# Attention rows of the second token half: one merged row of 128 scores in place of 256

## The chip, the cores and the metric

The kernel runs on one NeuronCore of a Trainium2 chip. Five engines work side by side, each through its own queue in order: TensorE (PE in the profile, with its weight loads as PEld), VectorE (DVE), ScalarE (ACT), GpSimd (POOL) and SyncE (SP, which issues most DMAs). They meet through semaphores only. The metric is device time in microseconds (us); less is better. A time is the median of several runs; the profile is one more execution, taken by the hardware profiler.

## The reference, cut to what matters

Two layers over 256 tokens of width 2048: a Mamba-2 mixer and then a sliding-window attention with 32 query heads of 64 channels, 4 shared key/value heads, a window of 128 and one sink per head. Both end in a layer norm of `ALPHA * x + mixer(x)`. The change touches the attention alone:

```python
def _swa_sink_attention(q, k, v, sinks):
    bsz, seqlen, hk, rq, hd = q.shape
    nb = seqlen // WINDOW                                   # 2 blocks of 128
    ...
    kk = jnp.concatenate([jnp.pad(kb, pad)[:, :-1], kb], axis=2)   # block before, own block
    vv = jnp.concatenate([jnp.pad(vb, pad)[:, :-1], vb], axis=2)
    s = jnp.einsum("bcqhrd,bckhd->bchrqk", qb, kk).astype(jnp.float32) * (hd ** -0.5)
    qi = jnp.arange(WINDOW)[:, None] + WINDOW
    ki = jnp.arange(2 * WINDOW)[None, :]
    diff = qi - ki
    ...
    valid = (diff >= 0)[None] & (diff < WINDOW)[None] & (kpos >= 0)
    s = jnp.where(valid[None, :, None, None], s, -jnp.inf)
    ...
    m = jnp.maximum(jnp.max(s, axis=-1, keepdims=True), sk)
    p = jnp.exp(s - m)
    p = p / (jnp.sum(p, axis=-1, keepdims=True) + jnp.exp(sk - m))
    o = jnp.einsum("bchrqk,bckhd->bcqhrd", p.astype(vv.dtype), vv)
```

For a query at place q of the second half (tokens 128 to 255), a key at place k of its own block is valid where k <= q, and a key at place k of the block before is valid where k > q. So exactly 128 of the 256 scores of a row are valid, and for each k exactly one of the two blocks holds the valid one. The first half has only its own block.

## The kernel before, in words

All matmul operands are float32, and the large products are made of three matmuls each: weights and activations are split into a high part and a remainder, and high*high, high*low and low*high are added up in PSUM (`mac`, `x_stat`, `out_unit`). Weights arrive as units of 128x2048 floats in two DMAs; ScalarE writes the high part of each half (L135), VectorE the remainder (L136). `next_unit` loads two units ahead of use.

The first layer takes the span up to about 690 us and is not touched. The second starts with K and V (x_stat, then `ktr` turns K), then follows a list of steps `B_ORDER` over the four KV heads j: "q" (`q_block`, four units, L744 to L746), "g" (`gate_block`, four units of 48 matmuls each, L208), "o" (`out_unit`, four units of 24 matmuls each, L268 to L270). The output units of the last head come at the very end, followed by the layer norm.

The attention itself is cut into small steps which are laid between these units by a list written out by hand: `later(n, fn)` puts a step on the list, and each unit ends in `tick()`, which counts the list down and emits the steps that are due, in their order on the list. For head j the steps are: `qtr` (turn the rotated queries, L799), `attend(j, 0)` (first token half), and from inside it `turn_p` after 3 ticks, `pv` after 6 and `attend(j, 1)` after 3. `attend(j, 1)` asks for its own `turn_p` after 3 ticks and `pv` after 4. For the last head, `pv` of the first half comes after 4 ticks and `attend(3, 1)` after 1. The tile framework then puts the instructions of each engine in an order, mainly the program's, and adds the semaphore waits.

`attend(j, h)` works on 128 queries of 8 query heads. It makes scores with two tiles of PSUM at a time (L836, two rows of 64 partitions each, for even and odd heads), adds the mask while copying them to SBUF (L841, VectorE), takes the row maximum (L849), combines it with the sink (L850 to L852), runs eight exponentials on ScalarE, each with a row sum (L855), adds the sink's share (L858), inverts (L859) and multiplies all weights by it (L860). `turn_p` transposes the weights on TensorE, four 128x128 blocks to a PSUM tile (L869), and copies each tile to SBUF, on ScalarE (L874) for odd heads and VectorE (L876) for even ones. `pv` multiplies V with them (L883), applies the gate (L889) and splits the result (L898, L899) for the output units.

For h = 1 the row has 256 scores: L836 has 256 columns per head, `p1` is 128x8x256, and L869 runs 16 times per head j, into four PSUM tiles.

The PSUM ring `ax` has four tiles of 128x512 and serves all of these small steps: scores, transposes and the product with V. The ring `pt` in SBUF has four tiles too. `mask_a1` (columns 640 to 895 of the constants `cc`) is the mask of the second half, `mask_a0` (768 to 895) that of one's own block: 0 where k <= q and -1e30 elsewhere. Columns 256 to 383 of `cc` hold an upper triangle of ones, `tri` in `_layout`.

Of the kernel before, what the change touches and what calls it, by code (L numbers as in the profile page):

```python
# [8 lines left out]
F32 = mybir.dt.float32  # L9
F32R = mybir.dt.float32r  # L10
I32 = mybir.dt.int32
AF = mybir.ActivationFunctionType
ALU = mybir.AluOpType
AX = mybir.AxisListType

P = 128
# [29 lines left out]
NEG = -1.0e30  # L46
# [15 lines left out]
def trunk(ctx: ExitStack, tc: tile.TileContext, A: dict, out: bass.AP, dbg=None):  # L62
    nc = tc.nc
# [16 lines left out]
    def nm(s):  # L80
        uid[0] += 1
        return f"{s}_{uid[0]}"
# [4 lines left out]
    def ax_tile():  # L87
        return ax_ps.tile([P, 512], F32, tag="ax", name=nm("ax"), bufs=4)

    cc = cst.tile([P, 896], F32, tag="cc", name="cc")  # L90
    ident = cc[:, 0:128]
    ones = cc[:, 128:256]
    mask_ssd = cc[:, 256:640]
    mask_a1 = cc[:, 640:896]
    mask_a0 = cc[:, 768:896]
    pc = cst.tile([P, PC_END], F32, tag="pc", name="pc")
    eps_t = cst.tile([P, 1], F32, tag="eps", name="eps_t")
# [532 lines left out]
    for g in range(NG):  # L630
        t = 10 * g
# [84 lines left out]
    bp = pool("bp")  # L716
# [106 lines left out]

    def attend(j, h):

        nk = P * (h + 1)
        q2 = qT[j, h]
        p = bp.tile([P, 8, nk], F32, tag=f"p{h}", name=nm("p"), bufs=1)
        mask = mask_a1 if h else mask_a0
        per = 512 // nk  # L830
        for b in range(0, 4, per):
            pss = [ax_tile(), ax_tile()]
            for i in range(per):
                for par in range(2):
                    rows = slice(64 * par, 64 * par + 64)
                    nc.tensor.matmul(  # L836
                        pss[par][:, i * nk : (i + 1) * nk], q2[rows, b + i, :], kT[rows, j, :nk],
                        start=True, stop=True,
                    )
            for par in range(2):  # L840
                nc.vector.tensor_tensor(  # L841
                    p[:, par * 4 + b : par * 4 + b + per, :],
                    pss[par][:].rearrange("p (a k) -> p a k", a=per),
                    mask.unsqueeze(1).to_broadcast([P, per, nk]), ALU.add,
                )
        sk = snk[:, j * 8 : j * 8 + 8]
        sm = bp.tile([P, 8, 8], F32, tag="sm", name=nm("sm"), bufs=2)
        mx, ng, rs, es, ri = [sm[:, i, :] for i in range(5)]
        nc.vector.tensor_reduce(mx, p[:], AX.X, ALU.max)  # L849
        nc.vector.tensor_tensor(mx, mx, sk, ALU.max)  # L850
        nc.vector.tensor_scalar(ng, mx, -1.0, None, ALU.mult)
        nc.vector.tensor_tensor(es, sk, ng, ALU.add)  # L852
        nc.scalar.activation(es, es, AF.Exp)
        for r in range(8):
            nc.scalar.activation(  # L855
                p[:, r, :], p[:, r, :], AF.Exp, bias=ng[:, r : r + 1], accum_out=rs[:, r : r + 1]
            )
        nc.vector.tensor_tensor(rs, rs, es, ALU.add)  # L858
        nc.vector.reciprocal(ri, rs)  # L859
        nc.vector.tensor_tensor(p[:], p[:], ri.unsqueeze(2).to_broadcast([P, 8, nk]), ALU.mult)  # L860

        pts = {}

        def turn_p():
            for kc in range(h + 1):
                for par in range(2):
                    pt = ax_tile()
                    for a in range(4):
                        nc.tensor.transpose(  # L869
                            pt[:, a * P : (a + 1) * P], p[:, par * 4 + a, kc * P : (kc + 1) * P], ident  # L870
                        )
                    t = bp.tile([P, 512], F32, tag="pt", name=nm("pt"), bufs=4)
                    if par:
                        nc.scalar.copy(t[:], pt[:])  # L874
                    else:
                        nc.vector.tensor_copy(t[:], pt[:])  # L876
                    pts[kc, par] = t

        def pv():
            ov = ax_tile()  # L880
            for kc in range(h + 1):
                for par in range(2):
                    nc.tensor.matmul(  # L883
                        ov[64 * par : 64 * par + 64, :], vt[:, kc, j * 64 : j * 64 + 64], pts[kc, par][:],
                        start=kc == 0, stop=kc == h,
                    )
            o = bp.tile([P, 4, P], F32, tag="o", name=nm("o"), bufs=1)
            hs = slice(h * P, (h + 1) * P)
            nc.vector.scalar_tensor_tensor(  # L889
                o[:], ov[:].rearrange("p (a t) -> p a t", a=4), 0.5, sg[j][:, :, hs], ALU.mult, ALU.mult  # L890
            )
            if j not in os_:
                os_[j] = (
                    bp.tile([P, 4, S], F32R, tag="oH", name=nm("oH"), bufs=2),
                    bp.tile([P, 4, S], F32R, tag="oL", name=nm("oL"), bufs=2),
                )
            oH, oL = os_[j]
            nc.scalar.activation(oH[:, :, hs], o[:], AF.Copy)  # L898
            nc.vector.tensor_tensor(oL[:, :, hs], o[:], oH[:, :, hs].bitcast(F32), ALU.subtract)  # L899

        last = j == 3
        later(3, turn_p)
        later(4 if last or h else 6, pv)
        if h == 0:
            later(1 if last else 3, lambda: attend(j, 1))
# [65 lines left out]
def _layout(inputs):  # L971
    import numpy as np

    f = {k: np.asarray(v) for k, v in inputs.items()}
    c = np.ascontiguousarray
    a = {}
    x = f["x"][0]
    a["xt"] = c(x.T.reshape(KT, P, S).transpose(1, 0, 2))
    a["xk"] = c(x.reshape(2, P, D).transpose(1, 0, 2))

    def wstat(w):
        k, n = w.shape
        return c(w.reshape(k // P, P, n // P, P).transpose(2, 1, 0, 3).reshape(n // P, P, k))

    def xstat(w, per, n):
        k, m = w.shape
        return c(
            w.reshape(k // (per * P), per, P, m // n, n).transpose(3, 0, 2, 1, 4).reshape(-1, P, per * n)
        )

    w = f["a_w_in"][0]
    o_xs, o_b, o_c, o_dt = DI, 2 * DI, 2 * DI + 1024, 2 * DI + 2048
    order = []
    for g in range(NG):
        blk = [o_b + g * P, o_c + g * P]
        blk += [o_xs + g * 512 + i * P for i in range(4)]
        blk += [g * 512 + i * P for i in range(4)]
        order += [blk[k] for k in (BLOCKS0 if g == 0 else BLOCKS)]
    cols = np.concatenate([np.arange(s, s + P) for s in order])
    a["wa"] = wstat(w[:, cols])  # L1000
    wdt = w[:, o_dt:].reshape(KT, P, NHD).transpose(1, 0, 2)
    a["first"] = np.concatenate([a.pop("xt"), a["wa"][0].reshape(P, KT, P), wdt], 2)
    conv = np.concatenate([f["a_conv_w"][0], f["a_conv_b"]], 0)
    corder = []
    for g in range(NG):
        corder += [o_b - DI + g * P, o_c - DI + g * P] + [g * 512 + i * P for i in range(4)]
    cv = np.stack([conv[:, s : s + P] for s in corder], 0).transpose(2, 0, 1).reshape(P, 240)
    dsk = np.repeat(f["a_d"][0], 64).reshape(32, P).T
    nw = f["a_norm_w"][0].reshape(32, P).T
    two = lambda v: np.concatenate([v, v])[:, None]  # L1010
    a["pc"] = c(np.concatenate([cv, dsk, nw, two(f["a_dt_bias"][0]), two(f["a_log"][0])], 1))
    wo = f["a_w_out"][0]
    a["wo"] = xstat(wo, 4, 512).reshape(4, NG, P, 2048).transpose(1, 0, 2, 3).reshape(32, P, 2048)
    a["lng"], a["lnb"] = f["ln_g"], f["ln_b"]
    a["wkv"] = xstat(f["kv_w"], 4, 512)
    a["kvb"] = f["kv_b"]
    wi = f["b_w_in"][0]
    a["wq"] = xstat(wi[:, :D], 4, 512)
    a["wg"] = wstat(wi[:, D:])
    a["qb"] = f["b_q_bias"][0]  # L1020
    a["snk"] = f["b_sinks"][0].reshape(4, 4, 2).transpose(0, 2, 1).reshape(32)
    wb = f["b_w_out"][0]
    a["wb"] = xstat(wb, 4, 512).reshape(4, 4, P, 2048).transpose(1, 0, 2, 3).reshape(16, P, 2048)
    a["pos"] = c(f["positions"][0].reshape(2, P).T)
    inv = (np.float64(500000.0) ** (-np.arange(0, 16, 2) / 16.0)).astype(np.float32)
    a["inv"] = np.tile(inv[None], (P, 1))
    i = np.arange(P)
    cc = np.zeros((P, 896), np.float32)
    cc[:, 0:128] = np.eye(P)
    cc[:, 128:256] = 1.0  # L1030
    tri = (i[None, :] >= i[:, None]).astype(np.float32)
    cc[:, 256:384] = tri
    cc[:, 384:512] = 1.0
    cc[:, 512:640] = tri
    cc[:, 640:768] = np.where(i[None, :] > i[:, None], 0.0, NEG)
    cc[:, 768:896] = np.where(i[None, :] <= i[:, None], 0.0, NEG)
    a["cc"] = cc
    return {k: c(v) for k, v in a.items()}
# [20 lines left out]
```

## Time and profile before

| | |
|---|---|
| median of 3 runs | 1021.66 us (1019.65 to 1025.03) |
| profiled execution, time | 1019.52 us |
| profiled execution, span from first to last instruction | 1017.7 us |
| granted TensorE clock, mean | 0.998 |
| HBM read | 195.41 MB, 194 GB/s over the span |
| transposes of weights, L869 | 96, of which 64 in the second halves |
| scores, L836 | 128 matmuls, 64 of 128 columns and 64 of 256 |

A line of the groups reads: source line, engine, operation, output <- inputs, shapes, count, then busy time in us and the mean of one in ns, then the idle time of the engine before them and what ended it. A line of the stretches gives, for each engine, its busy time in that window in us and its number of instructions. Matmul records overlap, so a record's length is not what it takes from the queue; the distance from one start to the next is.

### The profile page before, as it was taken

To read this page: it belongs to the slowest core of one execution; us is meant where nothing else is said; L and a number is where in the kernel's file an instruction comes from. 1 tells how busy PE (TensorE), PEld (TensorE's weight loads), DVE (VectorE), ACT (ScalarE), POOL (GpSimd) and SP (SyncE) were. 2 spreads that over 40 slices of the span, in tenths; PEclk is the share of its full clock that TensorE was granted. 3 is DMA by queue.
4 is the path that set the end of the run, shared out by engine and by line. 5 is a ranking of instruction groups with operands and counts; after the bars stand their busy time and mean duration, and the time that the engine had idled before them with its cause. 6 is when DMAs were issued, how large, how long until landed. Compare 5 with 4: busy or idle time off the path is not lost.

```text
span 1017.7 us, 17576 instructions
## 1 busy us (share of the span) xinstructions
PE 1001.8 (98%) x7012; PEld 900.8 (89%) x7012; DVE 772.2 (76%) x1099; ACT 560.5 (55%) x917; POOL 89.8 (9%) x112
## 2 busy tenths in 40 slices
PE   8999999999999999999999999999999999999997
PEld 6999989999999998998999998868988879879875
DVE  5869887966786886786786786897567875775876
ACT  6686846647646655654664663545455453453632
POOL 0000303004003003001200301201000000000002
PEclk9999999999999999999999999999999999999999
DMA  8797676565675666666666456647545545545522
GB/s 318 265 289 250 192 248 203 175 226 168 201 225 186 215 204 187 214 207 194 200 199 207 156 194 193 245 148 237 179 164 176 163 141 179 177 137 180 203 84 83
DMA packets 57794, 198.79 MB, mean 195 GB/s; under 512 B 6304, under 2 KB 10928, under 8 KB 56944
## 3 DMA queue, kind: packets, MB, share of 16 engines
q1 hardware_dynamic: 56352, 191.61, 58.0%
q0 software_dynamic: 1072, 5.53, 1.5%
q8 instruction: 55, 0.90, 0.3%
q10 hardware_dynamic: 288, 0.52, 0.1%
q14 instruction: 27, 0.22, 0.1%
HBM read 195.41 MB, written 2.23 MB: 194 GB/s over the span
## 4 chain that ended last, share of the span: by engine, by line
PE 77%; DVE 9%; ACT 5%; DMA 5%; issue 3%; POOL 1%; SPq 0%; ACTq 0%; DVEq 0%; POOLq 0%
PE mm L208 40%; PE mm L268 7%; PE mm L269 7%; PE mm L270 7%; PE mm L744 3%; PE mm L745 3%; PE mm L746 3%; DVE wl L136 3%; ACT wh L135 2%; DMA wr<-in_wa 2%; DVE cv L389 1%; PE ax L506 1%; DMA rb<-rscr 1%; PE ax L836 1%; PE ax L883 1%
## 5 line engine op out<-in xcount | busy, mean ns | idle before, releaser
L136 DVE TENSOR_TENSOR wl<-wr,wh 128x1024 fp32r<-128x1024 f32 (+2 forms) x342 | 398.3, 1181 | 132.3 <-ACT wh L135 131.1
L135 ACT ACTIVATE wh<-wr 128x1024 fp32r<-128x1024 f32 (+2 forms) x342 | 337.4, 1011 | 237.4 <-PE mm L208 74.3
L208 PE MATMUL mm<-xH,wh 128*128 128x256 f32 x1280 | 356.6, 279 | 2.2 <-DVE cv L389 1.8
L208 PE MATMUL mm<-xH,wl 128*128 128x256 f32 x1280 | 355.0, 277 | 1.5 <-DVE wl L136 1.5
L208 PE MATMUL mm<-xL,wh 128*128 128x256 f32 x1280 | 354.9, 277 | 0.0
L208 PEld LDWEIGHTS mm<-xH,wh 128*128 128x128 f32 x1280 | 241.0, 188 | 6.8 <-issue 2.6
L208 PEld LDWEIGHTS mm<-xH,wl 128*128 128x128 f32 x1280 | 240.9, 188 | 2.1 <-DVE wl L136 1.9
L208 PEld LDWEIGHTS mm<-xL,wh 128*128 128x128 f32 x1280 | 241.1, 188 | 0.9
L268 PE MATMUL mm<-wh,yH 128*128 128x512 f32 x256 | 101.4, 396 | 0.0
L269 PE MATMUL mm<-wh,yL 128*128 128x512 f32 x256 | 99.9, 390 | 0.0
L270 PE MATMUL mm<-wl,yH 128*128 128x512 f32 x256 | 99.7, 389 | 0.0
L522 POOL TENSOR_TENSOR yz<-yz,z 128x256 f32<-128x256 f32 x32 | 32.9, 1037 | 523.3 <-DVE yz L517 523.3
L389 DVE SCALAR_TENSOR_TENSOR cv<-mm,pc,cv 128x255 f32<-128x255 f32 x144 | 68.6, 476 | 6.4 <-ACT cv L387 5.0
L208 PE MATMUL mm<-x1H,wh 128*128 128x256 f32 x256 | 71.9, 281 | 0.0
L208 PE MATMUL mm<-x1H,wl 128*128 128x256 f32 x256 | 71.0, 277 | 0.0
L208 PE MATMUL mm<-x1L,wh 128*128 128x256 f32 x256 | 71.0, 277 | 0.0
L744 PE MATMUL mm<-wh,x1H 128*128 128x512 f32 x160 | 63.3, 396 | 0.0
L745 PE MATMUL mm<-wh,x1L 128*128 128x512 f32 x160 | 62.7, 392 | 0.2 <-DVE x1L L708 0.2
L746 PE MATMUL mm<-wl,x1H 128*128 128x512 f32 x160 | 62.6, 391 | 0.3 <-DVE wl L136 0.2
L268 PEld LDWEIGHTS mm<-wh,yH 128*128 128x128 f32 x256 | 48.1, 188 | 10.3 <-DVE z L459 1.0
L270 PEld LDWEIGHTS mm<-wl,yH 128*128 128x128 f32 x256 | 48.1, 188 | 10.1
L269 PEld LDWEIGHTS mm<-wh,yL 128*128 128x128 f32 x256 | 48.1, 188 | 9.0
(183 smaller groups left out, 1312.5 us busy)
## 6 DMA issues: line engine op xcount, KB each, us to landing
wr<-in_wa SPq DMA_DIRECT2D x158, 512.0 KB, 5.0
wr<-in_wo SPq DMA_DIRECT2D x64, 512.0 KB, 4.6
wr<-in_wq SPq DMA_DIRECT2D x32, 512.0 KB, 4.3
wr<-in_wg SPq DMA_DIRECT2D x32, 512.0 KB, 4.7
wr<-in_wb SPq DMA_DIRECT2D x32, 512.0 KB, 4.5
rb<-rscr SPq DMA_DIRECT2D x16, 512.0 KB, 5.6
el<-rscr SPq DMA_DIRECT2D x16, 256.0 KB, 5.0
wr<-in_wkv SPq DMA_DIRECT2D x8, 512.0 KB, 5.2
```

Of the source, the lines that this page charges most:

```text
L135: nc.scalar.activation(h[:, sl], v, AF.Copy)
L136: nc.vector.tensor_tensor(l[:, sl], v, h[:, sl].bitcast(F32), ALU.subtract)
L208: m = nc.tensor.matmul(ps, a, b, start=first and i == 0, stop=last and i == 2)
L268: nc.tensor.matmul(ps[:], aH[:, k, hs], u.h[:, ks], start=k == 0, stop=False)
L269: nc.tensor.matmul(ps[:], aL[:, k, hs], u.h[:, ks], start=False, stop=False)
L270: nc.tensor.matmul(ps[:], aH[:, k, hs], u.l[:, ks], start=False, stop=k == 3)
L389: nc.vector.scalar_tensor_tensor(a[:, sft:], ps[:, : S - sft], w(3 - sft), a[:, sft:], ALU.mult, ALU.add)
L506: nc.tensor.matmul(ps[64 * r : 64 * r + 64, cols], xd[:, c, r, :], e[:, 256:] if c else e[:, :256], start=c == 0, stop=c == 1,)
L522: nc.gpsimd.tensor_tensor(v, v, st.z[i][:], ALU.mult)
L744: nc.tensor.matmul(ps[:], x1H[:, kk, hs], u.h[:, ks], start=kk == 0, stop=False)
L745: nc.tensor.matmul(ps[:], x1L[:, kk, hs], u.h[:, ks], start=False, stop=False)
L746: nc.tensor.matmul(ps[:], x1H[:, kk, hs], u.l[:, ks], start=False, stop=kk == KT - 1)
```

## The change

For the second token half, `p1` shrinks to 128x8x128. The scores are still made for both key blocks. ScalarE copies those of one's own block from PSUM into `p`, and VectorE then copies those of the block before over them wherever `mask_a0` is not zero (k > q): `copy_predicated` with the mask's bits as condition. Maximum, exponentials and scaling run over 128 places. `turn_p` transposes 8 blocks in place of 16 into two PSUM tiles, and VectorE copies each tile twice, once times `1 - tri` (the weights of the block before) and once times `tri` (those of one's own block), so that `pv` has the same four tiles and the same eight matmuls (four with each block's V) as before. The first half keeps its instructions; only the order of the loops in `turn_p` is turned round. In the constants, `1 - tri` takes the place of the first half of `mask_a1`.

```diff
-    mask_a1 = cc[:, 640:896]
+
+    tri, anti = cc[:, 256:384], cc[:, 640:768]
     mask_a0 = cc[:, 768:896]
...
-        p = bp.tile([P, 8, nk], F32, tag=f"p{h}", name=nm("p"), bufs=1)
-        mask = mask_a1 if h else mask_a0
+        p = bp.tile([P, 8, P], F32, tag=f"p{h}", name=nm("p"), bufs=1)
...
             for par in range(2):
-                nc.vector.tensor_tensor(
-                    p[:, par * 4 + b : par * 4 + b + per, :],
-                    pss[par][:].rearrange("p (a k) -> p a k", a=per),
-                    mask.unsqueeze(1).to_broadcast([P, per, nk]), ALU.add,
+                v = p[:, par * 4 + b : par * 4 + b + per, :]
+                if h == 0:
+                    nc.vector.tensor_tensor(
+                        v, pss[par][:].rearrange("p (a k) -> p a k", a=per),
+                        mask_a0.unsqueeze(1).to_broadcast([P, per, P]), ALU.add,
+                    )
+                    continue
+                two = pss[par][:].rearrange("p (a c k) -> p a c k", a=per, c=2)
+
+                nc.scalar.copy(v, two[:, :, 1, :])
+                nc.vector.copy_predicated(
+                    v, mask_a0.bitcast(U32).unsqueeze(1).to_broadcast([P, per, P]), two[:, :, 0, :]
                 )
...
-        nc.vector.tensor_tensor(p[:], p[:], ri.unsqueeze(2).to_broadcast([P, 8, nk]), ALU.mult)
+        nc.vector.tensor_tensor(p[:], p[:], ri.unsqueeze(2).to_broadcast([P, 8, P]), ALU.mult)
...
         def turn_p():
-            for kc in range(h + 1):
-                for par in range(2):
-                    pt = ax_tile()
-                    for a in range(4):
-                        nc.tensor.transpose(
-                            pt[:, a * P : (a + 1) * P], p[:, par * 4 + a, kc * P : (kc + 1) * P], ident
+            for par in range(2):
+                pt = ax_tile()
+                for a in range(4):
+                    nc.tensor.transpose(pt[:, a * P : (a + 1) * P], p[:, par * 4 + a, :], ident)
+                for kc in range(h + 1):
+                    t = bp.tile([P, 512], F32, tag="pt", name=nm("pt"), bufs=4)
+                    if h:
+                        nc.vector.tensor_tensor(
+                            t[:].rearrange("p (a q) -> p a q", a=4), pt[:].rearrange("p (a q) -> p a q", a=4),
+                            (anti, tri)[kc].unsqueeze(1).to_broadcast([P, 4, P]), ALU.mult,
                         )
-                    t = bp.tile([P, 512], F32, tag="pt", name=nm("pt"), bufs=4)
-                    if par:
+                    elif par:
                         nc.scalar.copy(t[:], pt[:])
                     else:
                         nc.vector.tensor_copy(t[:], pt[:])
...
-    cc[:, 640:768] = np.where(i[None, :] > i[:, None], 0.0, NEG)
+    cc[:, 640:768] = 1.0 - tri
```

More of the change, by code (lines that the diff above doesn't have):

```diff
@@ L11 @@
 I32 = mybir.dt.int32
+U32 = mybir.dt.uint32
 AF = mybir.ActivationFunctionType
```

## The prediction

> **What bounds the kernel now.** I read the page first, then busy time by stretches of the span, then the chain of waits, then the groups by shape and the timelines of single engines around the attention steps.
>
> ```profile
> span 1017.7 us, 17576 instructions
> PE 1001.8 (98%) x7012; PEld 900.8 (89%) x7012; DVE 772.2 (76%) x1099; ACT 560.5 (55%) x917; POOL 89.8 (9%) x112
> ...
> core 0: us, PE busy (x) PEld busy (x) DVE busy (x) ACT busy (x) POOL busy (x), PEclk, DMA share, GB/s
> ...
> 745.00:772.00 27.00, 26.89 (x133) 21.69 (x133) 21.30 (x28) 14.18 (x33) 0.00 (x0) 1.00 0.45 145
> 772.00:800.00 28.00, 28.00 (x239) 25.50 (x236) 18.18 (x39) 14.57 (x34) 0.54 (x1) 1.00 0.53 172
> 800.00:827.00 27.00, 26.98 (x131) 21.23 (x130) 23.39 (x31) 13.94 (x29) 0.00 (x0) 1.00 0.43 135
> ...
> 957.00:985.00 28.00, 27.05 (x129) 20.31 (x129) 22.86 (x32) 15.58 (x33) 0.29 (x1) 1.00 0.58 205
> ```
>
> The whole span is 98% TensorE, but the change touches the second layer alone, so its own stretches count. There TensorE is busy for 28.00 of 28.00 us and 26.98 of 27.00, at granted clock 1.00. VectorE is second with up to 23.39 of 27 (87%), ScalarE has half, DMA 43 to 58%. One stretch lacks 0.95 us (27.05 of 28). The waits of TensorE in the last third show why:
>
> ```profile
> PE ax L869 <- DVE o L889: 1.0, 1, 1.0
> PE ax L948 <- ACT dg L938: 0.9, 1, 0.9
> ```
>
> Two waits are all that its matmuls show, and one sits at the transposes of the attention weights (L869), the line that the change thins out. So here a TensorE instruction that disappears is worth its place in the queue, and work on VectorE or ScalarE is worth nothing until it makes TensorE wait.
>
> **TensorE: what goes.** For each of four KV heads the second token half has 16 transposes, after the change 8. Scores (L836) and the product with V (L883) keep their counts. The chain of waits shows the places; its columns are start, duration and what ran.
>
> ```profile
> 772.82 1.90 PE ax L869 x16
> ...
> 827.31 1.90 PE ax L869 x16
> 829.21 0.24 PE mm L744
> ...
> 882.83 0.88 PE ax L869 x8
> ...
> 903.87 1.90 PE ax L869 x16
> ...
> 968.86 1.04 PE ax L869 x8
> 969.93 0.68 DVE xr L277
> 970.61 0.61 DVE o L889
> 971.27 0.66 PE ax L869 x4
> 971.93 0.23 PE mm L268
> ```
>
> Sixteen take 1.90 us and are followed at once by projections (829.21). Eight, in the row at 882.83, take 0.88. A head therefore gains 1.90 - 0.88 = 1.02 us, three heads 3.06. If half of 1.90 is the better price for what stays, it is 0.95 each, 2.85.
>
> The last head is different. Its sixteen span 968.86 to 971.93, 3.07 us, because they need four PSUM buffers of the four in the "ax" ring while the output of the first half's PV product still holds one; the fourth set of four waits for VectorE to read that output (L889), which is itself behind a residual add (L277). After the change two buffers are enough, so the wait has no cause left: 3.07 - 0.88 = 2.19 us, or 2.03 if the eight take the 1.04 of the row at 968.86.
>
> Sum on TensorE: 3.06 + 2.19 = 5.25 us; by the lower values 2.85 + 2.03 = 4.88.
>
> **VectorE and ScalarE: what changes beside it.** The groups by shape over the last third:
>
> ```profile
> L855 ACT ACTIVATE p<-p,sm 128x256 f32<-128x256 f32 x32 | 15.8, 496 | 21.8 <-DVE sm L851 21.8
> L841 DVE TENSOR_TENSOR p<-ax,cc 128x512 f32<-128x512 f32 x24 | 15.3, 679 | 1.3 <-PE ax L836 1.3
> L855 ACT ACTIVATE p<-p,sm 128x128 f32<-128x128 f32 x32 | 12.4, 388 | 16.6 <-DVE sm L851 16.6
> L869 PE MATMUL ax<-cc,p 128*128 128x128 f32 x96 | 12.2, 275 | 1.0 <-DVE o L889 1.0
> L860 DVE TENSOR_TENSOR p<-p,sm 128x2048 f32<-128x2048 f32 x4 | 9.2, 2290 | 0.1
> L849 DVE TENSOR_REDUCE sm<-p 128x8 f32<-128x2048 f32 x4 | 9.1, 2283 | 0.1
> L820 DVE SCALAR_TENSOR_TENSOR sg<-sg,mm 128x256 f32<-128x256 f32 x16 | 6.5, 405 | 1.6 <-ACT sg L819 1.4
> L874 ACT COPY pt<-ax 128x512 f32<-128x512 f32 x12 | 6.5, 573 | 0.0
> L819 ACT ACTIVATE sg<-mm 128x256 f32<-128x256 f32 x16 | 5.9, 367 | 0.0
> L860 DVE TENSOR_TENSOR p<-p,sm 128x1024 f32<-128x1024 f32 x4 | 4.9, 1217 | 0.0
> L849 DVE TENSOR_REDUCE sm<-p 128x8 f32<-128x1024 f32 x4 | 4.8, 1208 | 0.0
> ```
>
> Per head, in the second half: the row maximum goes from 2.283 to 1.208 us and the scaling by 1/sum from 2.290 to 1.217, both because the first half already runs these at 1024 elements. The eight exponentials go from 0.496 to 0.388 us each, 0.86 in all on ScalarE. The four masked evictions of 512 scores (0.679 each) become four ScalarE copies of 256 and four predicated VectorE copies of 256. The ScalarE copy is priced by the activation that reads 256 from PSUM, 0.367, with 0.573 (512 elements) as its upper end. The trace has no predicated copy. Its nearest row is L820, 256 elements with one PSUM operand, 0.405; as upper end I take 0.679, the same work at twice the elements. I use 0.405, since the number of elements and the operands are L820's. The four transposed evictions all go to VectorE as masked multiplies of 512 PSUM elements, which is L841's shape at 0.679; before, two were there and two on ScalarE at 0.573.
>
> VectorE per head: -1.075 - 1.073 + 4 x (0.405 - 0.679) + 2 x 0.679 = -1.89 us (-0.79 at the upper end). ScalarE: 4 x 0.367 - 2 x 0.573 - 0.86 = -0.54 (+0.29 at the upper end). Neither engine is the bound, so this counts as nothing; what it needs is that no result is later for TensorE than now. Two such results exist.
>
> First, the scaled weights before the transposes:
>
> ```profile
> 820.08 2.29 DVE L860 TENSOR_TENSOR p<-p,sm 128x2048 f32<-128x2048 f32 x1
> ...
> 964.86 2.29 DVE L860 TENSOR_TENSOR p<-p,sm 128x2048 f32<-128x2048 f32 x1
> ```
>
> They are ready at 822.37 for transposes at 827.31 (4.9 us early), and in the last head at 967.15 for 968.86 (1.7 early). The maximum, exponentials and scaling on that way get 3.0 us shorter together, more than the extra ScalarE step per buffer adds (0.367 and 0.405 in place of 0.679, one pair overlapping the next).
>
> Second, the transposed weights before the PV product of the same half, in the first head:
>
> ```profile
> 764.33 0.17 DVE L858 TENSOR_TENSOR sm<-sm 128x8 f32<-128x8 f32 x1 [4.01 <-ACT p L855]
> ...
> 781.20 1.22 DVE L136 TENSOR_TENSOR wl<-wr,wh 128x1024 fp32r<-128x1024 f32 x1 [2.04 <-ACT wh L135]
> ...
> 774.72 5.48 PE mm L208 x48
> 780.19 1.87 PE ax L883 x8
> ```
>
> One unit of projections, 5.48 us, lies between the transposes and the product; four evictions of 0.679 need 2.72. VectorE works here without a gap from 764.33 to 781.20 - 2.04 = 779.16. With 1.07 less for the scaling and 1.36 more for evictions that stretch would end at 779.45, and TensorE would arrive 1.02 earlier than 780.19, at 779.17. Even with the evictions at the very end of the stretch the wait is 0.3 us; further forward it is zero. I take zero and keep 0.3 for each head, 1.2, for the lower end.
>
> **Sum.** 5.25 us less, with 4.88 - 1.2 = 3.7 at the low end. The profiled execution has a span of 1017.7 and a time of 1019.52; it would become 1012.4 and 1014.3. The median of the three timed runs, 1021.66, lies 2.1 above that execution. On the scale of the median the forecast is 1021.66 - 5.25 = 1016.4.
>
> **The rivals.** A: each removed transpose gives back its recorded duration. The group row says 275 ns: 32 x 0.275 = 8.8, and the 0.95 us that TensorE lacks in the last stretch, 9.75 in all, hence 1011.9. Against it stands the row at 882.83, in which eight start and finish inside 0.88 us, since they overlap. The Trainium skill ("TensorE: Matmul & The Clock Gate", section "Part 4: PE-mode transpose") gives about 275 ns for one in a kernel, mostly access latency; the trace agrees on the length of the record, and by that figure taken as cost the answer would be this rival's.
>
> B: the four evictions on VectorE come later than the PV product wants them. Before, ScalarE took half of them alongside; now the PV product hangs on one queue that also holds weight splits, rotary pieces and residual adds. If the two extra evictions (1.36 us) delay each head's product in full, 4 x 1.36 = 5.4 goes back: 1021.8, no change; with half of it 1019.1. For it: the stretch without a gap. Against: the 5.48 us of cover.
>
> C, on the other side: the predicated copy must wait for the ScalarE copy into the same place, and both queues are served in order. ScalarE's weight splits come in runs:
>
> ```profile
> 764.20 4.13 ACT L135 ACTIVATE wh<-wr 128x128 fp32r<-128x128 f32 x6
> ...
> 806.10 2.00 ACT L135 ACTIVATE wh<-wr 128x1024 fp32r<-128x1024 f32 x2 [3.07 <-issue]
> ```
>
> If a copy lands behind such a run, VectorE stands still at the predicated copy, and behind it stand the low halves of the next weights (L136), for which TensorE waits. VectorE has 27.00 - 23.39 = 3.6 us free in the tightest stretch and 3.2 more by the shorter maximum, scaling and mask (1.075 + 1.073 + 1.10), so 6.8 per head. Waits of w per head cost 4 x (w - 6.8); they eat the gain from w = 8.1 and make it over 0.5% slower from 9.4. Four copies behind runs of 2.00 give w = 8.0, an unchanged time; all four behind 4.13 give 16.5 and +33.5 us. With two and two, w = 12.3, it is 4 x 5.5 - 5.25 = +16.8, hence 1038.5. Against it: ScalarE has half its time free, and the maximum that now stalls it (21.8 us over 32 exponentials) hurts nobody.
>
> **How the numbers follow.** A difference of 0.5%, 5.1 us, is about what a measurement of this kernel can tell from none; it puts the border at 1016.55, just above the forecast. Chances: forecast 0.60, A 0.12, B 0.15, C 0.13. Of the forecast's 0.60 I put 0.40 beyond the border and 0.20 within: its centre lies past it, and shorter chains can only help where TensorE still waits. Faster is 0.40 + 0.12 = 0.52, within 0.5% 0.20 + 0.15 = 0.35, slower 0.13. The range goes down to A, 1011.9, and up past B, to 1023.0, the forecast's spread of runs (1019.65 to 1025.03 now) included; C's 0.13 and some of A lie outside.
>
> **What the changed profile would show.** L869's transposes fall from 96 to 64, and each second half has one row of eight near 0.9 us; TensorE's wait for L889 is gone. Row maximum and scaling appear at 1024 elements only, near 1.2 us, the exponentials at 388 ns 64 times. Sixteen predicated copies at 0.41 us and sixteen ScalarE copies at 0.37 appear. TensorE stays above 98%. The forecast is wrong if TensorE shows waits of over 1 us for the evictions before the PV product (B), or VectorE's idle time before the predicated copies exceeds 6.8 us per head and TensorE waits for L136 (C), or the predicated copy costs well above 0.68.

## The result, and the profile after

| | before | after |
|---|---|---|
| median of 20 runs, us | 1022.24 | 1017.77 (1014.6 to 1020.75) |
| ratio to before | | 0.9958, 95% interval 0.9945 to 0.9971 |
| profiled execution: time, span, us | 1019.52, 1017.7 | 1019.71, 1017.9 |

The kernel is 0.42% faster, about 4.3 us (1022.24 x 0.0042), inside the 0.5% that was named as the border and inside the forecast range; the median lies 1.4 us above the forecast of 1016.4. The ratio leaves out two of the twenty runs of the kernel before, which took 1249.76 and 5735.45 us. Yet the two profiled spans differ by 0.2 us only, so the profile has to be read by parts. The lines are numbered anew: L208 is now L210, L268 to L270 are L270 to L272, L744 to L746 are L746 to L748, the scores are L838, the transposes L878, the PV product L896, its reading L902.

The first page lines of the changed kernel answer to those shown of before:

```profile
span 1017.9 us, 17523 instructions
PE 1000.6 (98%) x6980; PEld 900.4 (88%) x6980; DVE 765.8 (75%) x1107; ACT 558.6 (55%) x925; POOL 89.8 (9%) x112
```

32 TensorE instructions fewer (7012 to 6980), VectorE 6.4 us less busy, ScalarE 1.9. To see where the second layer begins and ends I took two landmarks out of TensorE's timeline: the eight transposes of K near its start and the four matmuls with which the last layer norm ends. Columns: start, duration, engine, line, operation, output and inputs, count. Before:

```profile
710.10 1.03 PE L771 MATMUL ax<-cc,kd 128*128 128x128 f32 x8
...
1009.52 3.40 PE L948 MATMUL ax<-t,dg 128*128 128x512 f32 x4 [0.90 <-ACT dg L938]
```

After:

```profile
715.78 1.03 PE L773 MATMUL ax<-cc,kd 128*128 128x128 f32 x8
...
1010.58 1.98 PE L961 MATMUL ax<-t,dg 128*128 128x512 f32 x4 [0.89 <-ACT dg L951]
```

From landmark to landmark it is 299.42 us before and 294.80 after: 4.62 less. In front of the first landmark the profiled execution of the changed kernel was 5.68 us later, and that hides the gain in the span. In that stretch every engine has the same instructions in the same order in both kernels; a run below shows that it is a matter of the execution.

Where the 4.62 come from shows at the transposes of the second half. TensorE's timeline before, first and last head:

```profile
771.74 1.08 PE L883 MATMUL ax<-pt,vt 128*64 128x512 f32 x4
772.75 1.97 PE L869 MATMUL ax<-cc,p 128*128 128x128 f32 x16
774.47 0.37 PE L208 MATMUL mm<-x1H,wh 128*128 128x256 f32 x1
...
780.12 1.94 PE L883 MATMUL ax<-pt,vt 128*64 128x512 f32 x8
...
967.78 1.08 PE L883 MATMUL ax<-pt,vt 128*64 128x512 f32 x4
968.79 1.53 PE L869 MATMUL ax<-cc,p 128*128 128x128 f32 x12
971.27 0.66 PE L869 MATMUL ax<-cc,p 128*128 128x128 f32 x4 [0.95 <-DVE o L889]
...
977.31 1.94 PE L883 MATMUL ax<-pt,vt 128*64 128x512 f32 x8
```

and after:

```profile
777.43 1.08 PE L896 MATMUL ax<-pt,vt 128*64 128x512 f32 x4
778.44 1.09 PE L878 MATMUL ax<-cc,p 128*128 128x128 f32 x8
779.29 0.37 PE L210 MATMUL mm<-x1H,wh 128*128 128x256 f32 x1
...
784.93 1.94 PE L896 MATMUL ax<-pt,vt 128*64 128x512 f32 x8
...
970.84 1.08 PE L896 MATMUL ax<-pt,vt 128*64 128x512 f32 x4
971.85 1.09 PE L878 MATMUL ax<-cc,p 128*128 128x128 f32 x8
...
978.37 1.94 PE L896 MATMUL ax<-pt,vt 128*64 128x512 f32 x8
```

From one PV product to the next the first head took 8.38 us (780.12 - 771.74) and takes 7.50, a gain of 0.88; the last head took 9.53 and takes 7.53, a gain of 2.00, and the wait in brackets is gone. The two heads between them gain 0.88 each, read in the same way. That is 3 x 0.88 + 2.00 = 4.64, all of the 4.62 within rounding. Every other piece between these places has the same length to 0.02 us in both traces. From the first transpose to the start of the projection behind them, the sixteen of the first head hold the queue for 1.72 us (774.47 - 772.75) and the eight for 0.85 (779.29 - 778.44).

From 720 us on the matmuls of the changed kernel show one wait, where those of before showed two:

```profile
PE ax L961 <- ACT dg L951: 0.9, 1, 0.9
```

No wait for the copies of the transposed weights is among them.

The groups by shape in the last third of the changed kernel:

```profile
L882 DVE TENSOR_TENSOR pt<-ax,cc 128x512 f32<-128x512 f32 x16 | 10.2, 682 | 0.0
L870 DVE TENSOR_TENSOR p<-p,sm 128x1024 f32<-128x1024 f32 x8 | 9.8, 1220 | 0.1
L859 DVE TENSOR_REDUCE sm<-p 128x8 f32<-128x1024 f32 x8 | 9.7, 1215 | 0.1
L878 PE MATMUL ax<-cc,p 128*128 128x128 f32 x64 | 8.5, 276 | 0.0
L853 DVE COPY_PREDICATED p<-cc,ax 128x256 f32<-128x256 uint32 x16 | 5.8, 437 | 0.0
L852 ACT COPY p<-ax 128x256 f32<-128x256 f32 x16 | 5.4, 370 | 0.9 <-PE ax L838 0.8
```

The predicated copy takes 437 ns and VectorE never stands still in front of it (0.0 in the last column); the ScalarE copy takes 370.

### The profile page after: what moved, and what is told of

It is laid out like the page before. It is cut to its first block, busy times and chain, and to the rows that moved or that the text cites. A ratio compares the mean times of both kernels' runs of the same rounds, so it can differ in the third digit from the quotient of the medians.

```text
span 1017.9 us, 17523 instructions
## 1 busy us (share of the span) xinstructions
PE 1000.6 (98%) x6980; PEld 900.4 (88%) x6980; DVE 765.8 (75%) x1107; ACT 558.6 (55%) x925; POOL 89.8 (9%) x112
## 5 line engine op out<-in xcount | busy, mean ns | idle before, releaser
L210 PE MATMUL mm<-xH,wh 128*128 128x256 f32 x1280 | 357.4, 279 | 2.4 <-DVE cv L391 1.3
L210 PE MATMUL mm<-xH,wl 128*128 128x256 f32 x1280 | 355.7, 278 | 0.8 <-DVE wl L138 0.8
L210 PE MATMUL mm<-xL,wh 128*128 128x256 f32 x1280 | 356.0, 278 | 0.0
L210 PEld LDWEIGHTS mm<-xH,wh 128*128 128x128 f32 x1280 | 241.8, 189 | 7.1 <-ACT wh L137 2.3
L210 PEld LDWEIGHTS mm<-xL,wh 128*128 128x128 f32 x1280 | 242.1, 189 | 1.0
L210 PEld LDWEIGHTS mm<-xH,wl 128*128 128x128 f32 x1280 | 241.9, 189 | 1.0 <-DVE wl L138 1.0
L270 PE MATMUL mm<-wh,yH 128*128 128x512 f32 x256 | 102.2, 399 | 0.0
L272 PE MATMUL mm<-wl,yH 128*128 128x512 f32 x256 | 100.2, 391 | 0.0
L210 PE MATMUL mm<-x1H,wh 128*128 128x256 f32 x256 | 71.9, 281 | 0.0
L210 PE MATMUL mm<-x1H,wl 128*128 128x256 f32 x256 | 71.0, 277 | 0.0
L210 PE MATMUL mm<-x1L,wh 128*128 128x256 f32 x256 | 71.0, 277 | 0.0
L746 PE MATMUL mm<-wh,x1H 128*128 128x512 f32 x160 | 63.3, 396 | 0.0
L748 PE MATMUL mm<-wl,x1H 128*128 128x512 f32 x160 | 62.6, 392 | 0.3 <-DVE wl L138 0.2
L270 PEld LDWEIGHTS mm<-wh,yH 128*128 128x128 f32 x256 | 48.5, 190 | 10.4 <-DVE z L461 1.0
L272 PEld LDWEIGHTS mm<-wl,yH 128*128 128x128 f32 x256 | 48.4, 189 | 10.3
```

What stands on the lines that cost most here:

```text
L210: m = nc.tensor.matmul(ps, a, b, start=first and i == 0, stop=last and i == 2)
L270: nc.tensor.matmul(ps[:], aH[:, k, hs], u.h[:, ks], start=k == 0, stop=False)
L272: nc.tensor.matmul(ps[:], aH[:, k, hs], u.l[:, ks], start=False, stop=k == 3)
L746: nc.tensor.matmul(ps[:], x1H[:, kk, hs], u.h[:, ks], start=kk == 0, stop=False)
L748: nc.tensor.matmul(ps[:], x1H[:, kk, hs], u.l[:, ks], start=False, stop=kk == KT - 1)
```

## The experiments

Two theories stood against each other. T: the gain is TensorE time, the place of eight transposes per head in its queue and the ring wait of the last head. V: the gain comes from the shorter rows on VectorE and ScalarE, which bring everything behind them forward. All edits are against the changed kernel unless it is said otherwise. The table gives, for each, the way between the two landmarks, the way from the first landmark to the end of the span, and how long the last four matmuls took, all read as above.

| run | landmark to landmark, us | to the end, us | last four matmuls, us | ratio to before, interval |
|---|---|---|---|---|
| before | 299.42 | 307.60 | 3.40 | |
| after | 294.80 | 302.12 | 1.98 | 0.9958, 0.9945 to 0.9971 |
| e1_sixteen | 299.34 | 306.71 | 1.98 | 0.9993, 0.9978 to 1.0008 |
| e2_twice | 298.34 | 306.67 | 3.57 | 0.9991, 0.9975 to 1.0007 |
| e3_late_merge | 297.54 | 305.31 | 3.03 | 0.9989, 0.9969 to 1.0010 |
| e4_pred3 | 294.82 | 302.17 | 1.98 | 0.9945, 0.9925 to 0.9965 |
| e3b_late_merge_anti | 294.84 | 302.19 | 1.98 | 0.9947, 0.9928 to 0.9965 |
| e6_evict_twice | 299.48 | 307.78 | 3.68 | 0.9998, 0.9979 to 1.0017 |
| e5_scores_later | 292.98 | 300.34 | 2.51 | 0.9948, 0.9927 to 0.9968 |
| after_again | 294.84 | 302.87 | 3.25 | 0.9967, 0.9950 to 0.9984 |
| e5_again | 292.97 | 301.26 | 3.58 | 0.9945, 0.9922 to 0.9969 |

**Sixteen transposes again.** The rows stay short; only the transposes come back, into four tiles.

```diff
             for par in range(2):
-                pt = ax_tile()
-                for a in range(4):
-                    nc.tensor.transpose(pt[:, a * P : (a + 1) * P], p[:, par * 4 + a, :], ident)
                 for kc in range(h + 1):
+                    pt = ax_tile()
+                    for a in range(4):
+                        nc.tensor.transpose(pt[:, a * P : (a + 1) * P], p[:, par * 4 + a, :], ident)
                     t = bp.tile([P, 512], F32, tag="pt", name=nm("pt"), bufs=4)
```

> The changed kernel, but the second half again makes 16 transposes per head into four PSUM tiles (each block twice, one masked copy of each tile); rows stay 128 wide, VectorE and ScalarE keep their shorter work. Theory T (the gain is transposes, by their place in TensorE's queue, and the ring wait of the last head): the part from the K transposes to the end goes from 302.1 us back to about 306.8, with 0.9 us more in each of three heads and 2.0 in the last; ratio to the kernel before within 0.9985 to 1.0015. Theory V (the gain comes from the shorter rows on VectorE and ScalarE): the part stays at 302 to 303, ratio near 0.996.

Measured: 299.34 between the landmarks, 0.08 less than before the change, although VectorE and ScalarE keep all their savings. TensorE's timeline in the last head has the old wait back:

```profile
970.60 1.08 PE L896 MATMUL ax<-pt,vt 128*64 128x512 f32 x4
971.61 1.53 PE L879 MATMUL ax<-cc,p 128*128 128x128 f32 x12
974.66 0.66 PE L879 MATMUL ax<-cc,p 128*128 128x128 f32 x4 [0.82 <-DVE o L902]
```

Putting back the transposes and the tiles takes back the gain: T.

**The same transposes, two tiles.** Each is made twice into the same place.

```diff
-                for a in range(4):
+                for a in [0, 1, 2, 3] * (h + 1):
                     nc.tensor.transpose(pt[:, a * P : (a + 1) * P], p[:, par * 4 + a, :], ident)
```

> The changed kernel, but each of the 8 transposes of a second half is made twice into the same PSUM tile: 16 transposes, two tiles. Theory T: 0.88 us more per head in all four heads, 3.5 in all, and no wait of the last head's transposes for L902; the part from the K transposes to the end is 305.6, ratio about 0.999. The difference to the run with four tiles, about 1.1 us, is the ring wait alone. Theory V: no change to 302, ratio 0.996.

Measured: 298.34, that is 3.54 more than after (3.5 expected) and 1.00 less than with four tiles (1.1 expected). The sixteen of the last head run through:

```profile
970.06 1.08 PE L896 MATMUL ax<-pt,vt 128*64 128x512 f32 x4
971.07 1.97 PE L878 MATMUL ax<-cc,p 128*128 128x128 f32 x16
978.47 1.94 PE L896 MATMUL ax<-pt,vt 128*64 128x512 f32 x8
```

So of the 4.62 the transposes are 3.5 and the ring wait is 1.0; the two account for 4.54. To the end it was 306.67 and not 305.6, since the last four matmuls took 3.57 in place of 1.98 us; the ratio can't show the difference between these two runs.

**Long rows, merged late.** The kernel before, with rows of 256 up to the sum; then one addition, eight transposes, and copies times the triangle and minus that.

```diff
-        nc.vector.tensor_tensor(p[:], p[:], ri.unsqueeze(2).to_broadcast([P, 8, nk]), ALU.mult)
+        if h:
+            nc.vector.tensor_tensor(p[:, :, :P], p[:, :, :P], p[:, :, P:], ALU.add)
+        p = p[:, :, :P]
+        nc.vector.tensor_tensor(p, p, ri.unsqueeze(2).to_broadcast([P, 8, P]), ALU.mult)
...
+                for kc in range(h, -1, -1):
+                    t = bp.tile([P, 512], F32, tag="pt", name=nm("pt"), bufs=4)
+                    if h and kc:
+                        nc.vector.tensor_tensor(
+                            t[:].rearrange("p (a q) -> p a q", a=4), pt[:].rearrange("p (a q) -> p a q", a=4),
+                            cc[:, 256:384].unsqueeze(1).to_broadcast([P, 4, P]), ALU.mult,
+                        )
+                    elif h:
+                        nc.vector.tensor_tensor(t[:], pt[:], pts[1, par][:], ALU.subtract)
```

> The kernel before with its rows of 256 through mask, maximum, exponentials and sum; one VectorE addition of the two halves of a row then makes 128 weights, which are scaled, transposed 8 times per head and copied out twice (times the triangle, and the tile minus that). No predicated copy, no ScalarE copy of scores. Per head VectorE has 1.5 us more work than in the changed kernel. Theory T: as fast as the changed kernel, part from the K transposes to the end 302 to 302.6, ratio 0.9955. Theory V: most of the gain is lost, 305 to 307, ratio 0.999.

Measured: 297.54, 2.74 more than after, and 305.31 to the end: a miss for T, and within V's numbers. TensorE's timeline at the PV product of the second head shows something neither theory had:

```profile
834.69 1.07 PE L891 MATMUL ax<-pt,vt 128*64 128x512 f32 x2
835.69 0.49 PE L744 MATMUL mm<-wh,x1H 128*128 128x512 f32 x1
836.12 1.93 PE L891 MATMUL ax<-pt,vt 128*64 128x512 f32 x6
837.98 0.50 PE L745 MATMUL mm<-wh,x1L 128*128 128x512 f32 x1
```

The product is cut in two in TensorE's queue: two of its records, one projection matmul, the other six. In the changed kernel the eight stand together and the next projection starts 1.87 us after the first of them; here it is 837.98 - 834.69 = 3.29, of which one projection belongs to the other side. The product of the third head is cut in the same way. Each of the two costs 1.15 us; the other 0.44 lies in the last head, whose product stays together but takes 2.41 us in place of 1.94. The kernel's text asks for the eight matmuls one after another, and the framework orders the instructions before anything runs. That it puts other work in between where it reckons that an operand comes late is a guess; no run here shows its reckoning. The order was changed by the subtraction, which makes one copy wait for the other, or by the long rows; the next run separates these.

**Long rows, merged late, with the changed kernel's copies.** As before this, but the complement of the triangle is made once and the copies out are the two masked multiplies.

```diff
+    anti = bp.tile([P, P], F32, tag="anti", name="anti")
+    nc.vector.tensor_scalar(anti[:], cc[:, 256:384], -1.0, 1.0, ALU.mult, ALU.add)
...
+                for kc in range(h + 1):
+                    t = bp.tile([P, 512], F32, tag="pt", name=nm("pt"), bufs=4)
+                    if h:
+                        nc.vector.tensor_tensor(
+                            t[:].rearrange("p (a q) -> p a q", a=4), pt[:].rearrange("p (a q) -> p a q", a=4),
+                            (anti[:], cc[:, 256:384])[kc].unsqueeze(1).to_broadcast([P, 4, P]), ALU.mult,
+                        )
```

> As the late merge, but the two copies out of each PSUM tile are the changed kernel's masked multiplies (the complement of the triangle is made once on VectorE), so that the PV product's matmuls stand together in TensorE's queue as in the changed kernel. Theory T with the loss of the late merge put down to the split PV product (one projection matmul between its first and its last six records, 1.15 us in each of two heads): the part from the K transposes to the end is 302.1 to 302.6, or 303.0 to 303.5 where the last four matmuls run at the lower clock; ratio 0.9955. Theory V (long rows cost the time themselves): it stays near 305.3, ratio 0.999.

Measured: 294.84, as after to 0.04 us, with the PV products whole again and rows of 256 through maximum, exponentials and sum:

```profile
L857 ACT ACTIVATE p<-p,sm 128x256 f32<-128x256 f32 x32 | 15.8, 495 | 21.8 <-DVE sm L853 21.8
L851 DVE TENSOR_REDUCE sm<-p 128x8 f32<-128x2048 f32 x4 | 9.1, 2285 | 0.1
L873 PE MATMUL ax<-cc,p 128*128 128x128 f32 x64 | 8.5, 276 | 0.0
```

V falls: 64 transposes with long rows give the whole gain. The predicated copy and the ScalarE copies are not needed for it. The cut of the PV product came with the subtraction, then, and not with the long rows.

**Three predicated copies in place of one.** The same result with more work on VectorE.

```diff
-                nc.vector.copy_predicated(
-                    v, mask_a0.bitcast(U32).unsqueeze(1).to_broadcast([P, per, P]), two[:, :, 0, :]
-                )
+                for _ in range(3):
+                    nc.vector.copy_predicated(
+                        v, mask_a0.bitcast(U32).unsqueeze(1).to_broadcast([P, per, P]), two[:, :, 0, :]
+                    )
```

> The changed kernel with every predicated copy made three times, 8 more of 0.437 us per head on VectorE, 3.5 us per head. Theory T: VectorE is cover only, and the scaled weights are over 3 us early, so less than 0.5 us is lost: part from the K transposes to the end 302 to 302.6, ratio 0.996. Theory V: 4 x 3.5 us of VectorE work on the path, up to 14 us more; already a third of it, 4.7, would take the gain back.

Measured: 294.82. VectorE was busy 16.5 us with them in place of 5.8, which is 2.7 us more per head (less than the 3.5 expected, as records in a row overlap), and nothing moved:

```profile
L854 DVE COPY_PREDICATED p<-cc,ax 128x256 f32<-128x256 uint32 x48 | 16.5, 441 | 0.0
```

**Two copies of each transposed tile.** This measures the cover of rival B.

```diff
                     if h:
-                        nc.vector.tensor_tensor(
+                        for _ in range(2):
+                            nc.vector.tensor_tensor(
...
```

> The changed kernel with every masked copy of transposed weights made twice: 4 more of 0.68 us per head on VectorE, 2.4 us of its queue, between the transposes and the PV product. In the changed kernel the copies end 2.8, 1.8 and 1.3 us before the PV product (heads 0, 1, 3; head 2 as 1). Rival B's mechanism says that what exceeds this cover shows on TensorE: 0 + 0.6 + 0.6 + 1.1 us of waits, and more where the PV product is cut up in TensorE's queue, as it is in heads 1 to 3 of this kernel; 2.3 to 5 us, part from the K transposes to the end 304.4 to 307, ratio 0.998 to 1.0005. If cover doesn't matter: 302.1.

Measured: 299.48, 4.68 more; the gain is gone. To the end it is 307.78, past the 307 expected, with 3.68 us for the last four matmuls. The expected waits of 0.6, 0.6 and 1.1 us for the copies are not there. From 720 us on, the matmuls show the one wait that they show in the changed kernel:

```profile
PE ax L962 <- ACT dg L952: 0.9, 1, 0.9
```

What is there is the PV product in three pieces, second head:

```profile
833.46 1.07 PE L897 MATMUL ax<-pt,vt 128*64 128x512 f32 x2
834.46 0.50 PE L746 MATMUL mm<-wh,x1H 128*128 128x512 f32 x1
834.80 0.40 PE L747 MATMUL mm<-wh,x1L 128*128 128x512 f32 x1
835.12 1.08 PE L897 MATMUL ax<-pt,vt 128*64 128x512 f32 x4
...
837.03 1.07 PE L897 MATMUL ax<-pt,vt 128*64 128x512 f32 x2
838.03 0.50 PE L748 MATMUL mm<-wl,x1H 128*128 128x512 f32 x1
```

Heads 1, 2 and 3 (the second to the fourth) lose 1.54, 1.55 and 1.54 us; the first head, whose product stays whole, loses nothing. The doubled copies keep VectorE busy for 20.2 us in place of 10.2, which is 2.5 more per head. In the changed kernel the copies end 2.7 us before the product in the first head and 1.7, 1.7 and 1.3 before it in the others (0.1 less than expected in the first three), so the product is cut up in just those heads where the extra work is more than this cover.

The rows show what the cut costs. Where the kind of matmul changes, the next start comes 0.32 us after the last (834.80 to 835.12), in a run of projections 0.23. A pair of PV matmuls alone holds the queue for 1.00 (833.46 to 834.46), while eight together hold it for 1.87. The single starts tell why: in the whole product of the changed kernel (the row at 784.93) two matmuls start together, at 784.93, 785.41, 785.84 and 786.27; in the pair alone they start one after the other, at 833.46 and 833.94. Three pieces hold the queue for 1.00 + 1.01 + 1.00 us, 1.14 more than the whole, and the changes of kind add the rest. `pv` writes even and odd heads to different halves of the partitions in turn; that the two which start together are one of each is read from the program, not from the trace.

**The scores one tick later.** The prediction did not look at the scores of the second half. In heads 0 to 2 they stand right behind the first half's transposes, which hold tiles of the same ring; here one tick is put between.

```diff
-            later(1 if last else 3, lambda: attend(j, 1))
+            later(1 if last else 4, lambda: attend(j, 1))
```

> The changed kernel with the second half's attend(j, 1) one tick later for heads 0 to 2, so that its scores no longer follow the first half's transposes at once. There 16 score matmuls took 2.63 us, in the last head, where they stand alone, 1.93: TensorE waits 0.7 for two PSUM tiles of the ring that the transposes hold. Expected: 0.7 less in each of three heads minus one more change between kinds of matmul (0.1 to 0.2 each), 1.5 to 2.1 us less than the changed kernel: part from the K transposes to the end 300 to 300.6, ratio 0.9935 to 0.9945. If the ring wait is not the cause, no change: 302.1.

Measured: 292.98 in one execution and 292.97 in a second one, 1.82 less than after. In the changed kernel (first two rows: TensorE's timeline, first head) the scores behind the transposes take 2.79; here, alone, 2.00:

```profile
757.22 1.04 PE L878 MATMUL ax<-cc,p 128*128 128x128 f32 x8
758.19 2.79 PE L838 MATMUL ax<-kT,qT 64*128 64x256 f32 x16
```

```profile
755.90 1.04 PE L878 MATMUL ax<-cc,p 128*128 128x128 f32 x8
762.33 2.00 PE L838 MATMUL ax<-kT,qT 64*128 64x256 f32 x16
```

In the three heads the scores become 0.79, 0.71 and 0.70 us shorter, 2.20 in all; 0.38 is lost elsewhere, since the edit also moves the steps behind the scores by a tick and parts the second half's transposes from the PV product in front of them. The wait itself is in the trace: in the changed kernel the weight loads of the scores wait, at three places, 1.3 us in all for ScalarE's copy of a transposed tile (L887), and in this run they never do.

**Both once more.**

> The changed kernel unchanged, a second execution under the profiler. The part from the K transposes to the end: 302.1 us, or 303.0 if the last four matmuls run at the lower clock. The part before it has been anywhere from 708.9 to 715.8 in nine profiles of kernels whose first layer is the same instruction for instruction; if that is a matter of the execution, it is another value here than the 715.8 of the first profile, with the same waits in the second part. If the change itself had moved the first layer, it would be 715 to 716 again. Ratio 0.9945 to 0.997.

> The changed kernel with attend(j, 1) one tick later for heads 0 to 2, once more beside the changed kernel: part from the K transposes to the end 300.3 us, or 301.2 at the lower clock; 1.8 us less than the changed kernel in the same place, so a ratio about 0.0017 below that of the changed kernel, which the intervals of the two (some 0.002 each way) can't tell apart by themselves.

Measured: the changed kernel's first landmark is at 709.43 us in this execution, 6.35 earlier than in its first profile, and the way between the landmarks is 294.84 as against 294.80. So the first layer varies by itself, and the change did not touch it. The twenty runs of the changed kernel agree: their spans lie between 1012.8 and 1019.0 us. Four runs have 294.80 to 294.84 between the landmarks (after, after_again, e3b_late_merge_anti and e4_pred3), and their ratios go from 0.9945 to 0.9967; a ratio alone does not tell 0.2% here. Two runs of the version with later scores give 0.9948 and 0.9945 to before. It is the fastest kernel of this study by its traces; by the ratios alone, whose intervals overlap those of the changed kernel, it is not told apart.

## Why the prediction was right, point by point

**What bounds.** TensorE, as read: the changed kernel's second layer shortens by TensorE's own pieces (4.64 us by pieces, 4.62 by landmarks), and 2.7 us more of VectorE's time per head leave the same time.

**The transposes.** The mechanism was right and the size a little off: 5.25 us were forecast, 4.62 came. The mis-sized term is "1.90 - 0.88 = 1.02 us" per head. It is 0.88 in each of three heads, since the eight that stay are not those of the row at 882.83. Rows of the chain run from the end of the record before to the end of their own, so what stands in front counts. At 882.83 that was projections, and the eight took 0.88; the ones that stay come behind the PV product, and read in the same way they take 1.02 (from 777.43 + 1.08 to 778.44 + 1.09). From start to start sixteen take 1.72 and eight 0.85 in the very same place, and the difference, 0.87, is the gain that came. The price that the prediction set aside, 0.95, was nearer, and still too high. Eight of sixteen in one unbroken run cost 8 x 0.11.

**The last head.** Forecast 2.19 (or 2.03), measured 2.00. Of the 0.19 too much, 0.14 is the same term, the eight at 0.88 in place of 1.02; the other 0.05 was not traced to one place. The ring wait was read rightly: it returns with four tiles and is worth 1.00.

**VectorE and ScalarE.** The prices held: the predicated copy 437 ns for 405, the ScalarE copy 370 for 367, the masked copies out 682 for 679. VectorE saved 6.4 / 4 = 1.6 us per head, 1.89 were forecast; 0.13 of the difference is the dearer predicated copy (4 x 0.032). ScalarE saved 1.9 / 4 = 0.48, 0.54 were forecast. "Counts as nothing" was right, and more widely than argued: even the long rows cost nothing once the transposes are eight.

**Rival A** (275 ns for each transpose) is out: the record is 276 ns long, and its worth was 3.54 us over 32, 0.11 each. The Trainium skill ("TensorE: Matmul & The Clock Gate", section "Part 4: PE-mode transpose") gives about 275 ns for a 128x128 bf16 transpose within a kernel. The trace agrees on the length of the record, here with float32. **Rival B** did not happen here, and the experiment with doubled copies shows that a loss from late copies is real and near: 2.5 us more of VectorE's time per head take back everything. Its form was another than told: the order of the queue changes and the PV product is cut up, in place of a wait. **Rival C** did not happen: no idle time before the predicated copies. Its allowance of 6.8 us per head was too large, as it left out the two extra evictions; with the prediction's own net of 1.89 it is 3.6 + 1.89 = 5.5.

**The border.** The forecast lay 0.15 us past the 0.5% and the measured ratio, 0.9958, lies short of it; the 0.40 put beyond it and 0.20 within leaned the wrong way, since with 4.64 in place of 5.25 the forecast is 1017.0, within. The interval, 0.9945 to 0.9971, reaches past the border, so the ratio alone does not decide this; the trace does, with 4.62 of 1017.7 us, 0.45%. The range, 1011.9 to 1023.0, held an unchanged time too. That the median fell inside it says little; the rows and the runs above are what bears the forecast out.

## What to carry to other kernels

Where one engine is full, take the price of an instruction from one start to the next at the very place where it will stand, with its neighbours before and after: priced by a row of the same instruction behind other neighbours, the gain of a head came out 16% too large here (1.02 for 0.88). Look at the waits that the removed work caused, not only at its length: needing fewer tiles of the ring was worth more, in the one head that waited for them (1.00 us), than eight of the transposes (0.88). And where a framework orders the queues, work off the bounding engine can change that order and cost time without any wait in the profile: compare the order of the bounding engine's queue, not only its waits.

## What the runs showed that was not expected

The first layer varies from execution to execution with the same instructions: the first landmark lay at 708.9 to 715.8 us in eleven profiles, and at 715.78 and 709.43 for one and the same kernel. The second layer repeats to 0.04 us. Part of the difference is visible as waits; these are the longest ones of the whole span in the first and the second profile of the changed kernel:

```profile
PE mm L318 <- DMA first<-in_first: 3.7, 2, 3.5
PE ax L704 <- DVE xr L699: 3.4, 2, 3.1
```

```profile
PE mm L318 <- DMA first<-in_first: 3.4, 1, 3.4
PE ax L704 <- DVE xr L699: 1.9, 2, 1.6
```

These two lines make 1.8 us of the 6.35. The granted clock makes more: it is 0.66 from 62.5 to 67.5 us and 0.69 from 670 to 675.5 in the first profile, and 1.00 in both places of the second (59 to 64 and 665 to 670.5). From these figures I estimate its cost at 0.34 x 5 + 0.31 x 5.5 = 3.4 us. What moves the waits and the clock was not tried.

The last four matmuls took 1.98 us in four of eleven profiles and 2.51 to 3.68 in the others. In the two pairs of equal kernels these records differ by 1.27 and 1.07 us and the ends of the span by 0.75 and 0.92. The four come after TensorE has waited 0.9 us, and the granted clock of the stretch differs (last but two column); before and after:

```profile
1003.00:1018.00 15.00, 9.02 (x25) 4.38 (x23) 9.40 (x14) 2.97 (x7) 4.75 (x4) 0.85 0.36 140
```

```profile
1003.00:1018.00 15.00, 8.67 (x30) 4.95 (x28) 10.46 (x15) 4.03 (x8) 5.76 (x4) 0.94 0.36 140
```

In a stretch of 5.5 us around the four, the clock is 1.00 in the four profiles with 1.98 us and 0.64 to 0.72 in the seven others.

The Trainium skill ("TensorE: Matmul & The Clock Gate", section "Part 1: The HAM clock gate (the "warmup" mystery)") says that the clock is set by a window that runs freely and doesn't begin with the kernel. The several durations of the same four instructions agree with that; no run here shows the window itself.
